# Rotary swap transfers issued by GpSimd, and gate tiles split six and twelve around retention

## The chip, the core and the metric

The kernel runs on one core of one Trainium2 chip. The metric is the device time of one launch in microseconds. Most executions of a kernel agree within 0.3%.

## The reference, cut to what matters

Two transformer blocks in a chain on 512 tokens of width 1024, in fp32. The first (gated delta rule, dilated attention and an expert layer) is left as it is. The second has two layers, and each layer does this:

```python
for l in range(2):
    proj = rmsnorm(x) @ w_in[l]            # 1024 -> everything below
    (c_q, c_kv, k_pe, sb_q, sb_k, sb_v, r_q, r_k, r_v, r_g, gate_logits) = split(proj)
    y_a = causal softmax attention from the latents c_q, c_kv, k_pe
    y_b = stick_breaking_attention(sb_q, sb_k, sb_v)   # log_sigmoid of every score
    # rotary embedding on 8 heads of 64: the two halves of a head change places
    rope(x) = concat([x1 * cos - x2 * sin, x2 * cos + x1 * sin])
    y_c = retention(rope(r_q), rope(r_k), r_v)
    y_c = silu(r_g) * head_group_norm(y_c)
    gates = sigmoid(gate_logits)           # 3 branches x 1024
    x = x + sum_b(gates[b] * (y_b @ w_branch[l, b])) @ w_out[l]
    x = x + square(relu(rmsnorm(x) @ w_up[l])) @ w_down[l]
```

## The kernel before

Activations lie transposed, features on 128 partitions and the 512 tokens along the row. A projection is a chain of *units*. A unit takes one 128x1024 weight tile and computes 128 output features: 24 matmuls of 128x512, since every fp32 product is made of three (high by high, high by low, low by high part). The tile comes in by a DMA on SP's queue into `raw`; ScalarE rounds it to its high part (`whl<-raw` on ACT), VectorE subtracts to get the low part (`whl<-raw,whl` on DVE). The units take turns in two PSUM banks, and the epilogue that reads a unit's bank is issued in the middle of the next unit, so unit n+2 can't start before the epilogue of unit n. `tm_unit` is the token-major form for v: groups of 24 matmuls with 256 columns.

Beside this main stream run *side tasks*, written as generators: the pieces of the attentions, the rotary embeddings, retention. While the program is built, a planner (`tick`, `count`, `need`, with estimated clocks of PE, ACT and DVE) lets them issue a piece between the matmuls of the units. The order of each engine's instructions is then fixed, and each engine works through its own list in order: a DMA that an engine issues stands in that list too.

The order of the main stream in a layer of block 2 is the tuple `ORDER`: the latents ("c"), some gate tiles, the up-projections ("u"), stick-breaking ("sb"), more gate tiles, retention ("r"), and the rest of the gate tiles. A number is a count of gate units out of 24; each sends its result to DRAM (`gate`), from which it is read again when the branches are merged. "sb" ends by starting the task `sticks`, which takes a softplus of every score: Exp and Ln on ACT, in bursts. "r" (`retain`) projects q and k (four units each), then v (two `tm_unit`), then adds the tasks t1 = `rope_large(q)` and t2 = `rope_large(k)`, projects the four g tiles, and adds the task `retention`, which waits for t1, t2 and the softmax attention (job "a"). It first applies Silu to g, then works through four pairs of heads. Each pair ends in a chain: a mean by a matmul, subtract, square, a matmul, Ln, Exp, two multiplies.

When the gate units are done, the kernel waits for the jobs a, b and c, splits the twelve tiles of y into high and low parts, and starts the branch units (`w_b`). These can start only when the last chain of retention is through.

`rope_large` handles two tiles at a time. For each it copies the four groups of 32 partitions to a second tile with neighbours swapped, by four DMAs of 32x512 (64 KB each), then does three VectorE operations. That is 8 tiles and 32 DMAs in a layer, 64 in all. In the before kernel ScalarE issues them.

Of the kernel before, what the change touches and what calls it, by code (L numbers as in the profile page):

```python
# [74 lines left out]
AFTER = "a"  # L75
BRANCHES = ((0, 0), (0, 2), (0, 4), (1, 0), (1, 2), (1, 4), (0, 6), (1, 6))
ORDER1 = ("da0", "k", "q", "da1", "da2", "v", "z", 16)
ORDER = ("c", 6, "u", "sb", 8, "r", 10)
CONST_GROUPS = {"base": ("ident", "ones", "freq"), "dn": ("le", "ge", "nle", "nge"), "peer": ("iota",),
                "b2": ("lt", "nlt", "nge", "b64"), "b2r": ("ntri", "nones"), "rot": ("rotm",)}  # L80

# [66 lines left out]
def layouts(x, norm_mix, w_in, dn_conv, dn_a_log, dn_dt_bias, dn_out_norm, rel_bias, w_branch_dn,  # L148
# [45 lines left out]
    for l in range(2):  # L194
# [7 lines left out]
        n = o[10]  # L202
        for i, p in enumerate(ORDER):
            if isinstance(p, int):
# [52 lines left out]
def _pick(g, a, n):  # L257

    if g == 0:
# [6 lines left out]
        + ["w_br", "w_out1", "w_route", "u", "v"]  # L266
        + [n + l for l in "01" for n in [f"w_g{i}_" if isinstance(p, int) else "w_" + p for i, p in enumerate(ORDER)]
           + ["w_b", "w_o", "w_mlp"]])
# [42 lines left out]
class Prog:  # L311
# [1691 lines left out]
    def rope_large(self, lst, deps):  # L2003

        yield from self.until(*deps)
        yield from self.need(slots=7)
        cos, sin = self.rope_tabs(1)
        for i in range(0, len(lst), 2):
            yield from self.need(slots=5)
            bs = []  # L2010
            for x in lst[i:i + 2]:
                b = self.slot()
                for j in range(4):
                    k = j ^ 1
                    self.dma(b[32 * j:32 * j + 32], x[32 * k:32 * k + 32], self.nc.scalar)
                bs.append(b)
            yield 2
            for j, b in enumerate(bs):
                x, a = lst[i + j], self.slot()
                self.tt(b, b, sin, OP.mult)  # L2020
                self.tt(a, x, cos, OP.mult)
                self.tt(a, a, b, OP.add)
                self.put(b, x)
                lst[i + j] = a
            yield
        self.put(cos, sin)

    def layer(self, l, res):
# [127 lines left out]
        n = 0  # L2156
        for p in ORDER:
            if isinstance(p, int):
# [444 lines left out]
```

## Time and profile before

| | us |
|---|---|
| median of three runs | 3950.87 (3944.65 to 3953.07) |
| profiled execution, its own time | 3947.66 |
| its span in the trace | 3945.9 |
| PE busy | 3781.2 (96%) |
| DVE busy | 2543.5 (64%) |
| ACT busy | 1537.9 (39%) |
| POOL busy | 421.8 (11%), none of it in block 2 after its start |

Block 2 takes the second half of the span, its two layers being alike. Retention's stretch in the first layer is about 2310 to 2500 us, in the second about 3270 to 3470 us. In the timeline views a row gives the start, the time that a run of like instructions took, the engine, the line (L307 is a recording helper that issues nearly everything, L582 the DMA helper), and in brackets how long the engine stood idle before it and what released it. "ACTq" rows are DMAs that ScalarE issued.

### The profile page before, as it was taken

How to read it: one execution, taken by the hardware profiler on the slowest of the kernel's cores; microseconds unless marked ns; L12 is line 12 of the kernel's file. 1: busy time of each engine (PE TensorE's matmuls, PEld its weight loads, DVE VectorE, ACT ScalarE, POOL GpSimd, SP SyncE). 2: the span in 40 equal slices, each digit the busy share in tenths (PEclk: the TensorE clock that was granted, in tenths of full speed). 3: DMA queues.
4: the chain of work that ended last, by engine and by line, in shares of the span. 5: the costliest groups of instructions: out<-in, count | busy, mean ns of one | idle time of the engine just before them, and what ended most of it. 6: DMA issues, size and time to landing. Idle time of an engine off the chain costs nothing.

```text
span 3945.9 us, 56144 instructions
## 1 busy us (share of the span) xinstructions
PE 3781.2 (96%) x21866; PEld 3228.5 (82%) x21866; DVE 2543.5 (64%) x4608; ACT 1537.9 (39%) x2392; POOL 421.8 (11%) x460
## 2 busy tenths in 40 slices
PE   9999899999999979999999998999999997999998
PEld 6777777899889979999977776688888876678886
DVE  4565755699989878888766555653345564564334
ACT  3532334244545433333343443442233353243222
POOL 1010201020333532222100000000000000000000
PEclk9999999999999999999999999999999999999999
DMA  4232524376888979999832223432233222343222
GB/s 150 80 114 87 169 94 159 126 246 198 317 317 301 380 265 348 349 347 349 292 119 94 86 84 103 152 115 97 96 115 124 72 86 86 107 155 107 96 96 80
DMA packets 260139, 666.68 MB, mean 169 GB/s; under 512 B 27316, under 2 KB 105428, under 8 KB 256800
## 3 DMA queue, kind: packets, MB, share of 16 engines
q1 hardware_dynamic: 202752, 457.19, 34.1%
q0 software_dynamic: 53328, 200.61, 13.9%
q10 hardware_dynamic: 3792, 5.28, 0.5%
q8 instruction: 172, 2.82, 0.3%
q14 instruction: 95, 0.78, 0.1%
HBM read 576.16 MB, written 81.57 MB: 167 GB/s over the span
## 4 chain that ended last, share of the span: by engine, by line
PE 55%; DVE 3%; ACT 2%; DMA 1%; issue 1%; ACTq 1%; DVEq 0%
PE bank L307 55%; DVE s L307 1%; ACT s L307 1%; DVE big L307 1%; DVE whl L307 1%; ACTq L582 1%; ACT whl L307 1%; ACT big L307 0%; DMA s<-s 0%; DVE dbl L307 0%; DMA dbl<-big 0%; DMA big<-big 0%; DMA big<-decay 0%; DMA gate<-s 0%; DVE mla_m L307 0%
## 5 line engine op out<-in xcount | busy, mean ns | idle before, releaser
L307 PE MATMUL bank<-s,whl 128*128 128x512 f32 (+1 forms) x15156 | 3276.1, 374 | 116.5 <-DVE s L307 42.9
L307 PEld LDWEIGHTS bank<-s,whl 128*128 128x128 f32 x15156 | 2759.2, 190 | 530.6 <-issue 58.9
L307 DVE TENSOR_TENSOR whl<-raw,whl 128x1024 fp32r<-128x1024 f32 x651 | 795.1, 1222 | 516.5 <-ACT whl L307 511.2
L307 ACT ACTIVATE whl<-raw 128x1024 fp32r<-128x1024 f32 x651 | 682.9, 1055 | 696.7 <-PE bank L307 358.4
L307 DVE TENSOR_TENSOR big<-bank,big 128x512 f32<-128x512 f32 (+4 forms) x264 | 174.6, 665 | 288.1 <-PE bank L307 285.4
L307 DVE TENSOR_TENSOR s<-s,s 128x1024 f16<-128x1024 f16 (+9 forms) x498 | 296.4, 616 | 32.1 <-ACT s L307 20.5
L307 ACT ACTIVATE big<-big 128x512 f32<-128x512 f32 (+2 forms) x247 | 148.3, 612 | 364.5 <-DVE big L307 309.5
L307 ACT ACTIVATE big<-bank 128x512 f32<-128x512 f32 (+3 forms) x250 | 165.0, 707 | 287.8 <-PE bank L307 179.0
L307 ACT ACTIVATE s<-bank 128x384 f32<-128x384 f32 (+5 forms) x253 | 116.8, 487 | 368.4 <-PE bank L307 357.4
L307 PE MATMUL bank<-s,s 128*128 128x128 f16 (+12 forms) x2120 | 218.9, 266 | 6.7 <-DVE s L307 6.6
L307 ACT ACTIVATE s<-s 128x384 fp32r<-128x384 f32 (+7 forms) x303 | 155.1, 526 | 175.9 <-DVE s L307 162.3
L1701 POOL DMA_INDIRECT dbl<-rows_u,s x128 | 169.3, 1322 | 325.7 <-DVE dbl L307 139.3
L307 DVE SCALAR_TENSOR_TENSOR dbl<-dbl,dbl 128x1024 f32<-128x1024 f32 x128 | 154.5, 1217 | 10.6 <-DMA dbl<-rows_u,s 8.8
L307 DVE TENSOR_TENSOR s<-s,big 128x384 f32<-128x384 f32 (+5 forms) x265 | 127.6, 485 | 33.9 <-DMA big<-wd 18.5
L307 PEld LDWEIGHTS bank<-s,s 128*128 128x128 f32 (+4 forms) x1352 | 106.5, 147 | 42.9 <-issue 27.0
L307 ACT ACTIVATE s<-big 128x512 fp32r<-128x512 f32 (+3 forms) x144 | 94.5, 668 | 109.0 <-DVE big L307 107.0
L1701 POOL DMA_INDIRECT dbl<-rows_v,s x94 | 102.0, 1085 | 259.4 <-DVE dbl L307 252.4
L307 DVE TENSOR_TENSOR s<-bank,big 128x512 f32<-128x512 f32 (+4 forms) x151 | 90.5, 609 | 52.6 <-PE bank L307 50.1
L307 PE MATMUL bank<-whl,s 128*128 128x256 f32 (+1 forms) x816 | 112.6, 298 | 12.2 <-DVE s L307 12.2
L307 PEld LDWEIGHTS bank<-whl,s 128*128 128x128 f32 x816 | 106.3, 197 | 15.7 <-DVE s L307 13.1
L307 DVE SCALAR_TENSOR_TENSOR dbl<-dbl,s,dbl 128x1024 f32<-128x1024 f32 x93 | 118.8, 1278 | 0.0
L307 DVE SCALAR_TENSOR_TENSOR big<-bank,big 128x512 f32<-128x512 f32 x68 | 46.9, 690 | 103.0 <-PE bank L307 98.9
(259 smaller groups left out, 2034.3 us busy)
## 6 DMA issues: line engine op xcount, KB each, us to landing
raw<-u SPq DMA_DIRECT2D x128, 512.0 KB
raw<-v SPq DMA_DIRECT2D x128, 512.0 KB
raw<-w_mlp SPq DMA_DIRECT2D x128, 512.0 KB
wd<-big POOLq DMA_DIRECT2D x24, 1024.0 KB
big<-wd SPq DMA_DIRECT2D x48, 512.0 KB
raw<-w_g SPq DMA_DIRECT2D x48, 512.0 KB
s<-ga SPq DMA_DIRECT2D x112, 192.0 KB
raw<-w_da SPq DMA_DIRECT2D x36, 512.0 KB
```

Of the source, the lines that this page charges most:

```text
L307: return getattr(self.eng, f)(*a, **k)
L582: (eng or self.queue).dma_start(out, in_)
L1701: self.nc.gpsimd.indirect_dma_start(buf, None, self.I[table], bass.IndirectOffsetOnAxis(ap=idx, axis=0))
```

## The change

Two lines. In `ORDER`, the gate tiles between stick-breaking and retention go from 8 to 6, and those behind retention from 10 to 12. In `rope_large`, the swap DMAs are issued by GpSimd instead of ScalarE.

```diff
-ORDER = ("c", 6, "u", "sb", 8, "r", 10)
+ORDER = ("c", 6, "u", "sb", 6, "r", 12)
@@ rope_large
                 for j in range(4):
                     k = j ^ 1
-                    self.dma(b[32 * j:32 * j + 32], x[32 * k:32 * k + 32], self.nc.scalar)
+                    self.dma(b[32 * j:32 * j + 32], x[32 * k:32 * k + 32], self.nc.gpsimd)
```

No instruction is added or dropped. The planner interleaves the side tasks anew, from the gate units ahead of retention on.

The first place is ScalarE's list in layer 0, from the swaps of q's first two tiles on, before the change. The `s`, `big` and `dbl` names are tiles of the side tasks; `big<-bank` of 384 columns is the start of a softplus.

```order
L582 DMA dbl_21144<-s_20429 32x512 x4
L582 DMA dbl_21150<-big_74 32x512 x4
L307 ACTIVATE whl<-raw 128x1024
L307 ACTIVATE big_74<-bank_80 128x512
L582 DMA big_74<-big_74 32x512 x4
L582 DMA big_75<-big_75 32x512 x4
L307 ACTIVATE big_74<-bank_82 128x384
L307 ACTIVATE big_75<-bank_81 128x384
L307 ACTIVATE s_21235<-bank_79 128x384
L307 ACTIVATE s_21236<-bank_83 128x384
```

In the change, the same engine at the same place of layer 0, around the weight splits of the second and third gate tile behind "r":

```order
L307 ACTIVATE s_20808<-s_20808 128x512
L307 ACTIVATE s_20809<-s_20809 128x512
L307 ACTIVATE whl<-raw 128x1024
L307 ACTIVATE s_21207<-bank_83 128x512
L307 ACTIVATE big_74<-bank_81 128x384
L307 ACTIVATE s_21250<-bank_79 128x384
L307 ACTIVATE s_21257<-bank_82 128x384
L307 ACTIVATE s_21258<-bank_78 128x384
L307 ACTIVATE s_21281<-bank_80 128x512
L307 ACTIVATE s_21282<-bank_83 128x512
L307 ACTIVATE whl<-raw 128x1024
```

The DMA rows are gone from it, and a weight split stands ahead of the softplus bursts where the swaps stood.

The second place is GpSimd's list in layer 0 of the change. Before, its list ends with the first row here, a reload of the residual at the start of block 2, and two rows of program end.

```order
L582 DMA s_17818<-hres 128x512
L582 DMA s_21048<-dbl_20261 32x512 x4
L582 DMA dbl_21053<-s_20331 32x512 x4
L582 DMA dbl_20261<-s_20415 32x512 x4
L582 DMA s_21154<-s_20497 32x512 x4
L582 DMA s_21211<-dbl_20261 32x512 x4
L582 DMA s_21216<-big_74 32x512 x4
L582 DMA s_21271<-big_74 32x512 x4
L582 DMA s_21276<-big_75 32x512 x4
```

All 32 swaps of the layer stand in one queue with nothing between them.

The third place is TensorE's list at the end of layer 0's retention. `bank_76<-s,whl` is the last gate unit, `bank_82<-s,whl` (in the change `bank_81<-s,whl`) the first branch unit; the others are matmuls of the side tasks. Before:

```order
L307 MATMUL bank_83<-s_21939,big_74 128x512
L307 MATMUL bank_79<-s_21907,s_20868 64x512
L307 MATMUL bank_79<-s_21909,s_20868 64x512
L307 MATMUL bank_79<-big_75,s_20926 64x384 x2
L307 MATMUL bank_78<-big_74 128x512
L307 MATMUL bank_79<-dbl_21150,s_20958 64x256
L307 MATMUL bank_79<-dbl_21360,s_20958 64x256
L307 MATMUL bank_79<-s_21941,s_20996 64x128
L307 MATMUL bank_79<-s_21943,s_20996 64x128
L307 MATMUL bank_79<-big_75,big_74 128x512
L307 MATMUL bank_81<-big_75,big_74 128x512
L307 MATMUL bank_82<-s_21970,whl 128x512
```

And in the change:

```order
L307 MATMUL bank_80<-big_75,big_74 128x512
L307 MATMUL bank_83<-big_74 128x512
L307 MATMUL bank_76<-s_18248,whl 128x512
L307 MATMUL bank_76<-s_18249,whl 128x512
L307 MATMUL bank_76<-s_18248,whl 128x512
```

```order
L307 MATMUL bank_76<-s_18284,whl 128x512
L307 MATMUL bank_76<-s_18285,whl 128x512
L307 MATMUL bank_76<-s_18284,whl 128x512
L307 MATMUL bank_79<-big_74 128x512
L307 MATMUL bank_81<-s_21968,whl 128x512
```

Before, 35 matmuls of the side tasks stand between the last gate unit and the first branch unit; in the change one does, and the others lie among the matmuls of the gate units. Retention's heads begin in the sixth of twelve gate tiles behind "r" instead of the seventh of ten. Layer 1 has the same pattern.

## Rows read from the trace of the kernel before

**Rows 1.** The page: busy time by engine; the chain that ended last.

```profile
PE 3781.2 (96%) x21866; PEld 3228.5 (82%) x21866; DVE 2543.5 (64%) x4608; ACT 1537.9 (39%) x2392; POOL 421.8 (11%) x460
PE 55%; DVE 3%; ACT 2%; DMA 1%; issue 1%; ACTq 1%; DVEq 0%
```

**Rows 2.** Timeline of PE, layer 0: start us, us, instructions, idle before them.

```profile
2325.15 4.59 PE L307 MATMUL bank<-whl,s 128*128 128x256 f32 x24 [4.48 <-DVE s L307]
...
2386.16 6.11 PE L307 MATMUL bank<-s,whl 128*128 128x512 f32 x18 [11.72 <-DVE s L307]
...
2407.96 16.85 PE L307 MATMUL bank<-s,whl 128*128 128x512 f32 x72 [0.44 <-DVE dbl L307]
...
2478.53 0.95 PE L307 MATMUL bank<-s,s 64*128 64x128 f32 x4 [1.28 <-DVE s L307]
...
2490.80 1.13 PE L307 MATMUL bank<-big,big 128*128 128x512 f32 x2 [1.12 <-ACT big L307]
2493.36 1.12 PE L307 MATMUL bank<-big,big 128*128 128x512 f32 x2 [1.44 <-ACT big L307]
2496.45 0.79 PE L307 MATMUL bank<-s,whl 128*128 128x512 f32 x1 [1.96 <-ACT s L307]
2498.04 12.15 PE L307 MATMUL bank<-s,whl 128*128 128x512 f32 x43 [0.81 <-DVE s L307]
```

**Rows 3.** Timeline of PE, layer 1, the two longest waits.

```profile
3286.44 5.14 PE L307 MATMUL bank<-whl,s 128*128 128x256 f32 x24 [4.48 <-DVE s L307]
...
3352.98 5.73 PE L307 MATMUL bank<-s,whl 128*128 128x512 f32 x18 [15.48 <-DVE s L307]
```

**Rows 4.** Chain of waits, 2370 to 2400 us: start us, us, what.

```profile
2377.59 1.94 DMA s<-s
...
2383.30 0.96 ACT whl L307
2384.28 1.23 DVE whl L307
2385.51 0.60 DVE s L307
```

**Rows 5.** Timeline of ACT, layer 0: softplus burst, swaps, table load.

```profile
2314.31 0.52 ACT L307 ACTIVATE big<-big 128x384 f32<-128x384 f32 x1
...
2320.88 1.99 ACT L307 ACTIVATE whl<-raw 128x1024 fp32r<-128x1024 f32 x2
...
2362.64 5.01 ACTq L582 DMA_DIRECT2D big<-big  x8
2371.78 0.96 ACT L307 ACTIVATE big<-bank 128x384 f32<-128x384 f32 x2 [8.57 <-DVE big L307]
...
2374.37 5.10 ACTq L582 DMA_DIRECT2D s<-s  x8
...
2428.64 1.28 ACT L555 ACT_TABLE_LOAD   x1
```

**Rows 6.** Timeline of DVE: waits for transfers, block 2 and block 1.

```profile
2358.62 0.69 DVE L307 TENSOR_TENSOR dbl<-dbl 128x512 f32<-128x512 f32 x1 [4.04 <-DMA dbl<-s]
...
3322.37 0.69 DVE L307 TENSOR_TENSOR dbl<-dbl 128x512 f32<-128x512 f32 x1 [5.95 <-DMA dbl<-s]
...
481.39 0.69 DVE L307 TENSOR_TENSOR s<-s,s 128x512 f32<-128x512 f32 x1 [3.24 <-DMA s<-og]
```

**Rows 7.** Windows, layer 0: busy PE, PEld, DVE, ACT, POOL; PEclk; DMA share; GB/s.

```profile
2386.00:2390.00 4.00, 3.84 (x9) 3.07 (x10) 3.26 (x8) 2.43 (x4) 0.00 (x0) 0.51 0.00 0
2498.00:2502.00 4.00, 3.96 (x9) 3.14 (x10) 4.00 (x7) 4.00 (x8) 0.00 (x0) 0.50 0.77 226
```

**Rows 8.** Timeline of POOL, block 1: DMAs that GpSimd issues.

```profile
478.44 0.54 POOL L582 DMA_DIRECT2D s<-og  x1 [0.55 <-DVE dbl L307]
...
598.78 3.19 POOL L582 DMA_DIRECT2D big<-gd  x6
...
1460.97 0.56 POOL L582 DMA_DIRECT2D rope<-s  x1 [6.24 <-ACT s L307]
```

## The prediction, made before the changed kernel ran

> **What bounds the kernel now.** I read the page first. TensorE is busy 96% of the span and is the largest piece of the chain that ended last; no other engine has over 64% [rows 1]. The change adds no work to TensorE and takes none away, so it can only move TensorE's idle time and its clock. That idle time is the next thing to look for, in the timeline of PE through retention's stretch in both layers. In layer 0 it is in four places. One wait of 4.48 us stands in v's projection. One of 11.72 us stands ahead of a unit behind retention's projections. Two waits of about 0.5 us follow, of which one is shown. And the end of retention has five waits of 1.28, 1.12, 1.44, 1.96 and 0.81 us, 6.6 in sum; two more there, under 0.3 us each, are left aside [rows 2]. Layer 1 repeats the pattern row by row, but its long wait is 15.48 us [rows 3]. Together that is 23.7 and 27.5 us, 51.2 in all.
>
> What ends the long wait is read from the chain of waits and the timeline of ACT. The transfer of a swap arrives, ScalarE then works through a softplus burst, reaches the high part of the next weight tile at 2383.30, VectorE makes the low part at 2384.28 and the epilogue at 2385.51, and only that frees the bank that TensorE wants [rows 4]. Just ahead ScalarE issued eight swap DMAs in 5.01 us, waited 8.57 us until it could read the scores of the burst, and issued eight more in 5.10 us [rows 5]. Ten microseconds of an in-order engine went into issuing, with the weight split queued behind.
>
> The long waits also cost clock. Behind the one of layer 0, and at the start of the branch units, the granted clock is 0.51 and 0.50, the lower of the two levels (1.2 and 2.4 GHz) [rows 7]. Its price comes from the rows. Seventy-two matmuls take 16.85 us at the full clock, 0.234 each. So 18 should take 4.2 and took 6.11 in layer 0 and 5.73 in layer 1, and 43 should take 10.1 and took 12.15 [rows 2, 3]. That is 1.9, 1.5 and 2.1 us.
>
> **Part 1, the swaps leave ScalarE.** Per layer, 32 DMAs at 0.63 us (5.01 over eight) are 20 us of ScalarE's list [rows 5]. Most of that lies beside TensorE's work and costs nothing; the part that ends late is the long wait. With the DMA rows gone, the weight split stands ahead of the bursts and waits for nothing but its own tile and ScalarE's turn. I take the 11.72 and the 15.48 as gone: −27.2 us.
>
> GpSimd does nothing in block 2, so its issues cost no work of its own. Its price for an issue is 0.54 us, and six in a row took 3.19 [rows 8]: the 32 of a layer take 17 us. A transfer that it issues at 478.44 is used at 481.39, 2.95 us later [rows 6, 8]. So a pair of tiles needs 8 × 0.54 + 3 = 7.3 us, a little more than one unit (24 × 0.234 = 5.6 us). The rows before show two waits of VectorE for swaps, 4.04 and 5.95 us [rows 6], with no idle row of TensorE at either. So a swap that is late by a few microseconds has cover.
>
> The Trainium skill, "SBUF — State Buffer", section "SBUF: two separate sides", speaks against this part: GpSimd writes the descriptors of its DMAs itself, and can't while VectorE runs an operation in a mode with two ports. The Trainium skill, "SBUF — State Buffer", section "Who interferes with whom", says that TENSOR_TENSOR has no such mode. The row that bears on it is an issue of 0.56 us in a stretch where VectorE runs TENSOR_TENSOR [rows 8], so the trace agrees with the second sentence and no row of it shows the first.
>
> **Part 2, the gate split.** The two gate units taken from ahead of "r" move everything of retention 11 us earlier against the softplus bursts. So the wait in v's projection meets a later unit of that projection, but the same queue: a burst of softplus from 2314.31 on, then two weight splits until 2322.87 [rows 5]. I keep it, at 4.0 for 4.48: −0.5 a layer.
>
> At the end two more gate units lie beside the last heads of retention. In the order of the change one matmul of the side tasks stands between the last gate unit and the first branch unit, instead of 35. The waits of 1.28, 1.12 and 1.44 us are then inside the units and covered; what can't be covered is the last chain itself (Ln, Exp, then the high and low parts of y), 1.96 + 0.81 = 2.8 us [rows 2]. That is −3.8 a layer, −7.7 in all.
>
> Two places may get worse. First, the cosine and sine tables of k are fetched again on SP's queue while VectorE waits for them, and behind the six operations of that pair stands an epilogue of a gate unit. The bounds are 0 (as at the two covered waits) and 5.95 us, the longest wait of VectorE for such a transfer [rows 6]. Second, the Silu of the g tiles needs a table load of 1.28 us [rows 5], and another back to Exp and Ln, now nearer to a weight split. Its bounds are 0 and 4.48 us, what the burst in v's projection costs [rows 2]. I take 2.0 for each, nearer to zero because TensorE ran through both waits of VectorE before: +4.0 a layer, with the two small waits of 0.5 us gone in return, so +3.0.
>
> **Sum.** Idle: −27.2 − 1.0 − 7.7 + 6.0 = −29.9; with the small waits left aside, about −31. Clock: −1.9 − 1.5 at the long waits; at the branch units I expect most of 2.1 back in layer 0, and more than that in layer 1 where it also falls in the chain, together about −5. That is −8. In all −39 us. Against the profiled execution of 3947.66 us this gives 3909; it lies 3.2 us under the median of 3950.87, within the spread of the runs, and the median less 39 is 3911.9, of which I keep 3911.
>
> **The rivals.**
>
> *The issuer doesn't matter.* The wait could be the softplus bursts' own: the split that ends it comes behind eight activations as well as behind the DMAs [rows 4, 5]. Then the long waits stay, by another releaser, and only the tail improves: 7.7 us of idle time, 8.6 with the small waits left aside, and the 5 of clock at the branch units, 13.6 in all: 3937. For it: the wait of 4.48 us has a burst and no DMA in it. Against it: ten microseconds of issuing between 2362 and 2380. The Trainium skill, "DMA: Bandwidth & Descriptors", section "Issuing engines are not separate DMA queues", is on this rival's side: starting transfers on several engines saves only the sequencer's time to issue, usually small against the transfer. Here eight issues hold ScalarE for 5.01 us [rows 5] and the wait for the data behind them is 1.94 us [rows 4], so by the trace the issue is the larger part.
>
> *A new wait takes the old one's place.* The two new places cost near their upper bounds, 5 to 6 us each, not 2. Then +15 of idle time against my sum and the clock of two more waits, 4: 3911.9 + 19, about 3931.
>
> *Better.* If the softplus burst in v's projection is covered too and the new waits don't come, only 2.8 a layer stays of the 51.2: 46 us of idle time (47 with the small ones) and 12 of clock, 3892.
>
> *Slower: GpSimd's issues stretch.* This kernel would do so if an issue waits for the VectorE operations beside it. The place is the last pairs of k: between the ninth issue and the use of the last pair lie about five units, 28.5 us with the side work, in which 23 issues of p us and a landing of 4.5 (between 2.95 and 5.95 [rows 6]) must fit. The pair is late by 23p + 4.5 − 28.5, nothing at 0.54. About 2 us of lateness are covered, and part 1 and 2 gain 20 a layer, so the sign turns where 23p = 46, at p = 2.0. If each issue waited for two operations like a weight's low part (1.23 [rows 4]), p would be 3.0, the pair 45 us late, and each layer would lose 22.5: 3996. The Trainium skill, "SBUF — State Buffer", section "A bandwidth-pool intuition that's wrong (but worth ruling out)", gives about 3,100 ns for such a DMA beside a locking operation of VectorE, against 620 ns alone; taken for p, that would be 48 us late and about 4002. Against it: the issue row of 0.56 us, and that the rows of VectorE in this stretch are TENSOR_TENSOR [rows 4, 6, 8].
>
> **How the numbers follow.** The forecast has 62%. The issuer that doesn't matter has 10%, the new waits 10%, the better case 4%, the slower one 8%. A last 6% is for the slower mechanism at its point of balance, around p = 2, with a time within 0.2% of before. About 0.2%, 8 us, is what a measurement of this kernel can tell from no change. So faster has 0.62 + 0.10 + 0.10 + 0.04 = 0.86, same 0.06, slower 0.08. The range goes from 3896, where both new waits are zero and a little of the burst is covered too, to 3937, the first rival: the better, the same and the slower cases are left out, 18%.
>
> **What would show it.** After the change no wait of TensorE over 6 us in retention's stretch; the 4.48 still there at the end of a softplus burst; one wait of about 2 + 0.8 us before the branch units, without a clock of 0.5 behind the places where the long waits were; POOL rows of 32x512 swaps at 0.5 to 0.6 us each, VectorE waiting for them no longer than 6 us. The rival of the issuer is right if a wait over 8 us stands before the same units with ACT's burst as what holds the split. The prediction is wrong in its main term if POOL's issues take over 1.1 us each, or if the epilogue behind k's tables holds TensorE longer than the 5.95 us taken as its bound.

## The result, and the profile after

The changed kernel takes 3899.6 us (median of four, 3895.3 to 3900.8), against 3947.8 for the kernel before, run beside it. The ratio is 0.9882 with a 95% interval of 0.9869 to 0.9894: 1.2% faster, by 48 us. The forecast was 3911, in a range of 3896 to 3937.

Two lines of the page after answer to [rows 1]: TensorE has the same 21866 instructions, is busy 8.8 us less, and its share of the chain that ended last is 58% instead of 55%.

```profile
PE 3772.4 (97%) x21866; PEld 3221.4 (83%) x21866; DVE 2541.1 (65%) x4608; ACT 1536.9 (39%) x2392; POOL 457.6 (12%) x524
PE 58%; DVE 2%; ACT 2%; issue 1%; DMA 0%; DVEq 0%; ACTq 0%
```

In the timeline of PE after, these are all the waits of layer 0 in the stretch that [rows 2] shows of before, and the two longest ahead of the branch units of layer 1. Columns as in [rows 2].

```profile
2319.91 10.40 PE L307 MATMUL bank<-whl,s 128*128 128x256 f32 x72 [3.00 <-ACT s L307]
...
2375.05 4.33 PE L307 MATMUL bank<-s,whl 128*128 128x512 f32 x18 [0.95 <-DVE big L307]
...
2388.11 1.61 PE L307 MATMUL bank<-s,whl 128*128 128x512 f32 x6 [0.53 <-ACT s L307]
...
2395.65 0.49 PE L307 MATMUL bank<-dbl,s 128*128 128x512 f32 x1 [0.21 <-ACT dbl L307]
...
2396.38 1.08 PE L307 MATMUL bank<-s,s 128*128 128x512 f32 x5 [0.23 <-DVE s L307]
...
2473.86 0.50 PE L307 MATMUL bank<-s,whl 128*128 128x512 f32 x1 [1.96 <-ACT s L307]
2475.46 24.76 PE L307 MATMUL bank<-s,whl 128*128 128x512 f32 x96 [1.09 <-DVE s L307]
...
3263.18 10.25 PE L307 MATMUL bank<-whl,s 128*128 128x256 f32 x72 [3.00 <-ACT s L307]
...
3319.05 4.36 PE L307 MATMUL bank<-s,whl 128*128 128x512 f32 x18 [1.83 <-DVE big L307]
```

The waits of 11.72 and 15.48 us [rows 2, 3] have become 0.95 and 1.83. The wait in v's projection is 3.00 instead of 4.48. Of the five at the end of retention the last two are left, 1.96 and 1.09.

The time is accounted for best from where block 2 starts on, since the first block is the same code in both kernels. Its first long run of matmuls starts 3.8 us earlier in the profiled execution of after than in that of before:

```profile
1995.51 17.26 PE L307 MATMUL bank<-s,whl 128*128 128x512 f32 x64 [9.78 <-DVE whl L307]
```

(before), and

```profile
1991.75 17.00 PE L307 MATMUL bank<-s,whl 128*128 128x512 f32 x64 [9.78 <-DVE whl L307]
```

(after). In the fourteen traces of this study that start lies anywhere between 1985.8 and 1997.7, so 3.8 us is scatter. From it to the end of the span block 2 takes 1950.4 us before and 1906.2 after, 44.2 less. The idle time of TensorE in it, added up from all rows of its timeline, falls from 58.6 to 22.5: 36.1. Nearly all of the rest, 8.1, is clock: PE's busy time times (1 − PEclk), added over windows of 4 us through retention's stretch in both layers (2270 to 2530 and 3230 to 3502 us), falls from 14.8 to 7.0, by 7.8. The table has the same sums for the experiments, each ratio against the kernel before, run beside it; the last three columns are from one trace each.

| kernel | time, us (median) | ratio to before | block 2 | PE idle in it | lost to clock |
|---|---|---|---|---|---|
| before | 3947.8 | | 1950.4 | 58.6 | 14.8 |
| changed | 3899.6 | 0.9882 [0.9869, 0.9894] | 1906.2 | 22.5 | 7.0 |
| changed, once more | 3897.8 | 0.9881 [0.9865, 0.9896] | 1906.1 | 22.2 | 7.3 |
| GpSimd issues, split 8/10 | 3922.3 | 0.9941 [0.9923, 0.9959] | 1933.0 | 39.0 | 19.8 |
| ScalarE issues, split 6/12 | 3920.0 | 0.9930 [0.9911, 0.9949] | 1926.9 | 36.1 | 12.3 |
| SP issues, split 6/12 | 3899.6 | 0.9878 [0.9855, 0.9900] | 1905.0 | 23.1 | 6.3 |
| two DMAs for each swap | 3898.8 | 0.9881 [0.9865, 0.9898] | 1906.9 | 23.8 | 6.3 |
| four DMAs for each swap | 3955.9 | 1.0027 [1.0017, 1.0037] | 1965.9 | 63.7 | 24.2 |
| split 7/11 | 3908.7 | 0.9907 [0.9891, 0.9924] | 1917.6 | 33.0 | 11.3 |
| split 5/13 | 3893.2 | 0.9865 [0.9848, 0.9881] | 1902.3 | 25.0 | 5.0 |
| split 5/13, once more | 3895.7 | 0.9870 [0.9855, 0.9885] | 1902.5 | 25.1 | 5.2 |
| split 4/14 | 3905.6 | 0.9894 [0.9879, 0.9909] | 1910.3 | 29.2 | 4.9 |
| split 6/12, branch units of two attentions first | 3899.0 | 0.9879 [0.9863, 0.9896] | 1904.8 | 22.1 | 5.7 |
| split 5/13, branch units of two attentions first | 3914.0 | 0.9914 [0.9901, 0.9928] | 1918.5 | 32.2 | 9.5 |

### The profile page after: what moved, and what is told of

The parts are those of the page before. It is cut to its first block, busy times and chain, and to the rows that moved or that the text cites. A ratio compares the mean times of both kernels' runs of the same rounds, so it can differ in the third digit from the quotient of the medians.

```text
span 3898.0 us, 56154 instructions
## 1 busy us (share of the span) xinstructions
PE 3772.4 (97%) x21866; PEld 3221.4 (83%) x21866; DVE 2541.1 (65%) x4608; ACT 1536.9 (39%) x2392; POOL 457.6 (12%) x524
## 4 chain that ended last, share of the span: by engine, by line
PE 58%; DVE 2%; ACT 2%; issue 1%; DMA 0%; DVEq 0%; ACTq 0%
PE bank L307 58%; DVE s L307 1%; ACT s L307 1%; DVE big L307 1%; ACT whl L307 0%; DMA big<-rope 0%; DVE whl L307 0%; ACT L555 0%; ACT big L307 0%; DVE mla_m L307 0%; DVE dbl L307 0%; ACT dbl L307 0%; DVE bank L307 0%; DVEq L2598 0%; DVEq L307 0%
## 5 line engine op out<-in xcount | busy, mean ns | idle before, releaser
L307 ACT ACTIVATE s<-bank 128x384 f32<-128x384 f32 (+6 forms) x263 | 122.0, 489 | 414.1 <-PE bank L307 406.6
L307 PE MATMUL bank<-s,s 128*128 128x128 f16 (+10 forms) x2102 | 209.2, 260 | 4.6 <-DVE s L307 4.6
L582 POOL DMA_DIRECT2D s<-dbl x16 | 7.9, 500 | 1319.6 <-PE bank L307 1319.6
L307 PEld LDWEIGHTS bank<-s,s 32*32 32x32 f32 (+5 forms) x1334 | 104.4, 146 | 37.0 <-issue 26.2
L307 ACT ACTIVATE s<-big 128x512 fp32r<-128x512 f32 (+2 forms) x136 | 90.6, 677 | 106.7 <-DVE big L307 104.7
L307 PE MATMUL bank<-s,big 32*32 32x32 f32 (+6 forms) x960 | 121.2, 283 | 1.7 <-ACT big L307 1.3
```

The source lines that it names most:

```text
L307: return getattr(self.eng, f)(*a, **k)
L582: (eng or self.queue).dma_start(out, in_)
```

## Experiments: the two parts apart

**The issuer alone.** The split stays at 8 and 10:

```diff
-ORDER = ("c", 6, "u", "sb", 6, "r", 12)
+ORDER = ("c", 6, "u", "sb", 8, "r", 10)
```

(This diff and those below are against the changed kernel.)

> Only the issuer changes (GpSimd), the gate split stays 8 and 10; every engine's list but ScalarE's and GpSimd's is that of before. Theory (ScalarE's 20 us of issuing a layer ends the long wait): the waits of 11.72 and 15.48 us shrink under 4 us each, the end of retention keeps its waits (about 7 us a layer), the time falls by 25 to 32 us, near 3920. Rival (the softplus burst alone holds the weight split): a wait of 8 us or more stays at the same unit, the time falls by under 8 us.

It took 3922.3, 24 us less than before, just short of the 25 to 32 expected. Its timeline of PE has these waits in v's projection and at the unit where the long wait was, in layer 0 and in layer 1:

```profile
2316.16 5.49 PE L307 MATMUL bank<-whl,s 128*128 128x256 f32 x24 [4.48 <-DVE s L307]
2371.16 6.96 PE L307 MATMUL bank<-s,whl 128*128 128x512 f32 x18 [4.56 <-DVE s L307]
...
3327.91 6.50 PE L307 MATMUL bank<-s,whl 128*128 128x512 f32 x18 [4.76 <-DVE s L307]
```

The long wait shrinks by 7.2 and 10.7 us, but doesn't go, and stays above the 4 us expected. The chain of waits ahead of it, in order of time (start us, us, what), tells what is left:

```profile
2354.89 3.65 DMA big<-big
...
2365.96 2.34 ACT s L307 x5
2368.30 0.96 ACT whl L307
...
2369.28 1.23 DVE whl L307
2370.51 0.61 DVE s L307
```

The last of the softplus burst's activations (five in the second row), then the weight split, its low part and the epilogue: the tail of [rows 4] without the issues ahead of it. A swap's transfer is still in the chain (first row): VectorE waits 3.08 us for it, works off the pair and then reads the scores, and ScalarE, idle for 7.82 us, begins the burst only at 2361.39. So the first rival had a part of it right: with no issue left in ScalarE's list, the burst and what the burst waits for still cost TensorE 4.6 us. And the clock did not improve: 18 matmuls behind a wait of 4.56 us take 6.96 us, no less than the 6.11 behind 11.72 [rows 2]. Over the stretch this kernel loses more to the clock than before, 19.8 for 14.8; why more was not settled.

**The split alone.**

```diff
-                    self.dma(b[32 * j:32 * j + 32], x[32 * k:32 * k + 32], self.nc.gpsimd)
+                    self.dma(b[32 * j:32 * j + 32], x[32 * k:32 * k + 32], self.nc.scalar)
```

> Only the gate split changes (6 and 12), ScalarE issues the swaps. Theory (the two parts are separate): waits of about 8 to 16 us a layer stay between v's projection and retention's heads, the end of retention keeps only about 3 us, the time falls by 12 to 18 us, near 3934. Rival (two units more of distance are enough by themselves): no wait over 5 us, the time within 8 us of the changed kernel's 3900.

It took 3920.0, 27 us less than before, more than the 12 to 18 expected. The wait in v's projection is 3.00 in each layer, as in the changed kernel; with the issuer alone it stayed at 4.48. The end of retention has 3.0 us left in each layer, as expected. Between v's projection and the heads the waits are 7.1 us in layer 0 (a little under the 8 to 16 expected) and 10.2 in layer 1 in sum, of which these are the ones of layer 0 above 1 us:

```profile
2371.82 7.33 PE L307 MATMUL bank<-s,whl 128*128 128x512 f32 x24 [1.77 <-DVE s L307]
2384.16 6.93 PE L307 MATMUL bank<-s,whl 128*128 128x512 f32 x18 [5.01 <-DVE big L307]
```

In its chain of waits ScalarE's issuing is a piece of its own: eight DMAs between two parts of one burst, with the weight split behind the second.

```profile
2369.11 1.39 ACT s L307 x3
...
2370.57 0.60 ACTq L582
2371.20 0.61 ACTq L582
...
2375.13 1.09 ACT s L307 x2
2376.22 0.96 ACT whl L307
```

So both causes are real, and either part alone leaves the other's wait. In block 2 the issuer alone gives 17.4 us, the split alone 23.5, both 44.2: nearly the sum (40.9). In idle time the two overlap (19.6 and 22.5 against 36.1), and in clock it is the other way: the issuer alone loses 5.0 more than before, the split alone 2.5 less, both 7.8 less.

## Experiments: the queue that issues

**SP in GpSimd's place.**

```diff
-                    self.dma(b[32 * j:32 * j + 32], x[32 * k:32 * k + 32], self.nc.gpsimd)
+                    self.dma(b[32 * j:32 * j + 32], x[32 * k:32 * k + 32], self.nc.sync)
```

> The changed kernel with the swaps on SP's queue instead of GpSimd's, where weight tiles, gate results and the cosine and sine tables are queued too. Theory (any engine that isn't ScalarE does, since weight tiles are fetched several units ahead): within 6 us of the changed kernel. Rival (SP's in-order list stands still while a swap waits for its tile, and the weight loads behind it come late): TensorE waits for raw tiles or their high parts, 5 to 15 us a layer, 10 to 30 us slower than the changed kernel.

3899.6, the changed kernel's time; block 2 at 1905.0. So nothing of the gain hangs on GpSimd; what counts here is that the issuer isn't ScalarE. SP needs 0.59 us for one, GpSimd 0.50 and ScalarE 0.60 (median by line, DMAs of 32x512 from one SBUF tile to another).

**The fourth rival's price.** Each swap in pieces of 8 rows, four times the issues for the same bytes (and in the second kernel of 16 rows, twice):

```diff
-                    self.dma(b[32 * j:32 * j + 32], x[32 * k:32 * k + 32], self.nc.gpsimd)
+                    for p in range(0, 32, 8):
+                        self.dma(b[32 * j + p:32 * j + p + 8], x[32 * k + p:32 * k + p + 8], self.nc.gpsimd)
```

> The changed kernel with each swap cut in four DMAs of 8x512 on GpSimd: 128 issues a layer instead of 32, the same bytes. At 0.5 us each the formula of the prediction has p at 2.0 per swap: the last pair 22 us late (23 x 2.0 + 4.5 - 28.5), some 20 us of wait a layer, about 40 to 50 us slower than the changed kernel, near 3945. Rival (an issue costs by its rows, so that a quarter of a swap costs a quarter of 0.5 us, or the pairs have more cover than five units): within 6 us of the changed kernel.

> The changed kernel with each swap cut in two DMAs of 16x512 on GpSimd: 64 issues a layer, p = 1.0 us per swap. By the formula of the prediction the last pair is in time (23 x 1.0 + 4.5 - 28.5 = -1): within 6 us of the changed kernel. Rival (every 0.5 us more per swap costs in proportion, as from 32 to 128 issues, where it cost 56 us): 15 to 20 us slower, near 3918.

Four pieces took 3955.9: slower than before the change. An issue costs nearly the same whatever its rows (0.508 us with 8, 0.484 with 16, 0.496 with 32), so p is 4 × 0.508 = 2.0. By line, the swaps of both layers, the two largest of four groups, min/median/max ns:

```profile
L582 POOL DMA_DIRECT2D s<-big x96: 502/508/511, 2376.6 to 3372.8; - x96
L582 POOL DMA_DIRECT2D s<-dbl x64: 502/508/536, 2331.4 to 3348.3; - x64
```

Its chain of waits in the stretch is GpSimd's issuing, and TensorE waits for the pairs one after the other:

```profile
2369.67 6.13 POOL s L582 x13
...
2382.10 4.05 DMA s<-big
...
2386.43 5.25 POOL s L582 x11
```

```profile
2373.85 8.56 PE L307 MATMUL bank<-s,whl 128*128 128x512 f32 x24 [3.62 <-DVE s L307]
2392.84 7.68 PE L307 MATMUL bank<-s,whl 128*128 128x512 f32 x24 [10.43 <-DVE s L307]
2406.17 6.45 PE L307 MATMUL bank<-s,whl 128*128 128x512 f32 x18 [5.66 <-DVE big L307]
```

The prediction's formula gives 22 us of lateness at p = 2.0 and, less 2 of cover, 20 of wait a layer; the idle time of block 2 is 41.2 above the changed kernel's, 20.6 a layer. What it left out is the clock, 17.2 us more (24.2 against 7.0), so the sign turns somewhat below p = 2. Two pieces (p = 1.0) took 3898.8, as the formula says: the cover of five units is used up only beyond that.

## Experiments: how far the gates should move

Two more splits, then a third:

```diff
-ORDER = ("c", 6, "u", "sb", 6, "r", 12)
+ORDER = ("c", 6, "u", "sb", 7, "r", 11)
```

> The changed kernel with seven and eleven gate units. In its order 24 matmuls of the side tasks stand between the last gate unit and the first branch unit. Theory: it lies between the two splits; the end of retention waits about 5 us a layer, v's projection and the unit behind it keep the 4.5 us waits of the kernel with only the issuer changed, which has the same distance but one unit; 8 to 18 us slower than the changed kernel, 3908 to 3918. Rival (the wait behind v's projection hangs on the burst's place by one unit): it goes as in the changed kernel, and only 3 to 5 us are lost.

3908.7, at the near end of the expectation. The end of retention waits 5.9 us in layer 0, and the wait where the long one was is back at 4.08 and 5.41: it hangs on the burst's place by one unit. The wait in v's projection was expected at 4.5 and is 2.21.

> The changed kernel with five gate units ahead of retention and thirteen behind it. In its order 80 matmuls of the side tasks stand between the last gate unit and the first branch unit, where the changed kernel has one: retention's heads begin later although it has more units behind it. Theory (what counts is how many of retention's matmuls lie among gate units): waits of about 8 to 14 us a layer at the end of retention instead of 3, lower clock behind them, 15 to 30 us slower than the changed kernel, 3915 to 3930. Rival (each unit behind retention covers more of it): 3900 or less.

3893.2 where 3915 to 3930 was expected: a miss. The order of the matmuls had been read as if those that no gate unit surrounds were lost time. They take as long as anywhere; what costs is the chain of ACT and DVE between them. That the pairs of heads run side by side here and cover one another's chains is the likely reason, and was not tested. In its timeline of PE the end of layer 0's retention has eight waits, 7.45 us in sum, of which the last three are

```profile
2470.32 1.13 PE L307 MATMUL bank<-big 128*128 128x512 f32 x2 [1.44 <-ACT big L307]
2473.41 0.79 PE L307 MATMUL bank<-s,whl 128*128 128x512 f32 x1 [1.96 <-ACT s L307]
2475.01 45.29 PE L307 MATMUL bank<-s,whl 128*128 128x512 f32 x191 [0.80 <-DVE s L307]
```

Against that the waits behind v's projection are gone, the one in it is 1.63, and the clock is lost for less time. These don't add up to a lead: over block 2 the idle time is 2.5 us more than in the changed kernel and the clock's loss 2.0 less, while block 2 is 3.9 shorter. With the same 8978 matmuls TensorE is busy there for 1864.5 us instead of 1870.7; the clock explains 2.0 of that, and what shortens the rest was not settled.

> The changed kernel once more, beside the next three on one chip: 3896 to 3903, its ratio to the kernel before 0.987 to 0.990.

> Five and thirteen gate units once more. If its lead over the changed kernel (6 us, of which 4 lie in block 2) is real: 3 to 8 us under the changed kernel in the same call. If it was the scatter of the first block: within 2 us.

> The changed kernel with four and fourteen gate units. In its order 74 matmuls of the side tasks stand in one piece late in retention, much as with five and thirteen. If distance from the softplus bursts goes on paying: 3893 or less. If it is used up, since the waits that are left belong to the end of retention (about 7.5 us a layer with five and thirteen): 3892 to 3898.

On one chip the changed kernel took 3897.8 (0.9881, 0.9865 to 0.9896), five and thirteen 3895.7 (0.9870, 0.9855 to 0.9885): the intervals overlap. In block 2 the lead is the same in both pairs of traces, 1906.2 and 1906.1 against 1902.3 and 1902.5, so some 4 us of 3900 are probably real, and too little for these runs to show. Four and fourteen takes 3905.6, outside both expectations (3893 or less, 3892 to 3898): the waits at the end of retention stay and smaller ones come in the middle of it.

**The last chain covered.** What is left at the end with six and twelve is the last chain, 1.96 + 1.09 us a layer. The branch units of the other two attentions don't need it:

```diff
-        self.wait(*(job[x] for x in "abc"))
-        ys = [[self.hilo(t) for t in y] for y in (ya, yb, yc)]
+        self.wait(*(job[x] for x in "ab"))
+        ys = [[self.hilo(t) for t in y] for y in (ya, yb)]
...
             for b in range(3):
+                if b == len(ys):
+                    self.wait(job["c"])
+                    ys.append([self.hilo(t) for t in yc])
                 w = self.get()
```

> The changed kernel, but the branch units of the softmax and the stick-breaking attention start without waiting for retention; only the first branch unit that reads retention's result waits for it and splits its tiles. Theory (what is left at the end is retention's last chain, 1.96 + 1.09 us a layer): that wait shrinks to about 1 us, the high and low part of the first tile, and the clock behind it stays up in layer 0; 4 to 8 us faster than the changed kernel, near 3894. Rival (the wait moves to the third branch unit, or the splits of eight tiles ahead of it take its place): within 3 us of the changed kernel.

3899.0, no gain. In its timeline of PE the wait has moved:

```profile
2472.75 10.96 PE L307 MATMUL bank<-s,whl 128*128 128x512 f32 x47 [0.29 <-DVE s L307]
2484.76 0.50 PE L307 MATMUL bank<-s,whl 128*128 128x512 f32 x1 [1.05 <-ACT s L307]
2486.95 23.22 PE L307 MATMUL bank<-s,whl 128*128 128x512 f32 x94 [1.69 <-DVE s L307]
```

0.29 + 1.05 + 1.69 is 3.03, the same sum, 48 matmuls later. The 11 us of branch work are filled on ScalarE by eight splits of y that now stand ahead of the chain and by three loads of its tables, since Sigmoid comes between the chain's Ln and Exp and what went before:

```profile
2469.90 2.18 ACT L307 ACTIVATE s<-big 128x512 fp32r<-128x512 f32 x4
2471.98 2.19 ACT L307 ACTIVATE s<-s 128x512 fp32r<-128x512 f32 x4
...
2478.13 1.28 ACT L555 ACT_TABLE_LOAD   x1
2479.42 0.69 ACT L307 ACTIVATE big<-bank,eps 128x512 f32<-128x512 f32 x1
...
2481.74 1.28 ACT L555 ACT_TABLE_LOAD   x1
```

> Five and thirteen gate units, and the branch units of the other two attentions not waiting for retention. Its order lets 44 matmuls of the side tasks in one piece ahead of the last branch units. If retention's last chains are what is left (7.5 us a layer) and 22 us of branch work can cover half: 6 to 10 us under five and thirteen alone, near 3885. If the wait only moves to the first branch unit that reads retention's result, as with six and twelve: within 3 us of five and thirteen alone.

With five and thirteen the same edit took 3914.0 (0.9914, 0.9901 to 0.9928), 18 us more than without it, a miss of both expectations. In block 2 the idle time is 7.1 us more than without it and the clock's loss 4.3 more, of 16.0; the end of layer 0's retention waits 11 us in sum instead of 7.45. Why the edit lengthens these waits was not settled. No version tried beats the changed kernel by more than the runs can tell.

## Why the prediction came out right, step by step

The time, the sign and the range held, and the mechanism was the one forecast. The sizes of its terms were less good than their sum.

- **The long waits, −27.2 expected.** They are gone; the 0.95 and 1.83 us that stand at that place now hang on k's tables and are counted below. But the prediction gave all of it to part 1, the issuer. The issuer alone takes 17.9 of it (11.72 to 4.56, 15.48 to 4.76), and the rest goes only when part 2 moves the burst by two units as well. The shares depend on the order: of all waits between v's projection and the heads (29.2 in both layers) the issuer alone takes 19.9, the split alone 11.8, both 24.6. The step that failed is "With the DMA rows gone, the weight split stands ahead of the bursts": the kernel with only part 1 has the burst ahead of the split. The forecast for both parts held because both were made.
- **The wait in v's projection, −1.0 expected.** It went from 4.48 to 3.00 in each layer, −3.0; the split alone gives the same 3.00.
- **The end of retention, −7.7 expected.** From 7.1 a layer, with the two small waits that the prediction left aside, to 3.05: −8.1. What stays is Ln, Exp and the split of y, as named, at 3.05 for 2.8.
- **The two new waits, +8.0 expected, less the small ones.** They came where they were looked for, at 0.95 and 1.83 for the tables of k, and 1.0 and 0.9 around the Silu: 4.6 in sum. Of these last, 0.4 in each layer stand behind the Silu's table loads; 0.5 in each come just ahead of them (at 2388.11, the first load at 2389.34), and what they wait for was not settled. The chain of waits of after shows the first:

```profile
2355.02 4.32 DMA big<-rope
...
2363.33 3.15 DVE s L307 x6
2366.50 0.60 ACT s L307
2367.09 0.96 ACT whl L307
...
2374.30 0.60 DVE big L307
```

 The transfer of the tables takes 4.32 us of the chain, VectorE stands idle for 4.57 us (5.46 in layer 1), and TensorE pays 0.95 (1.83) when the epilogue in the last row comes late. The second rival, with 5 to 6 us at each place, is out.
- **Clock, −8 expected.** 7.8 measured, most of it where it was forecast. By place, the sum of the table falls from 3.3 to 0 behind the long waits (−3.4 expected; 18 matmuls now take 4.33 and 4.36), from 7.8 to 4.3 at the end of retention and the branch units (−5 expected), and from 3.6 to 2.7 in v's projection (nothing expected). At the branch units of layer 0 none came back: the first row here, of after with the columns of [rows 7], has 0.55 where before had 0.50. In layer 1 it did in part (second row). The changed kernel's second trace has it the other way round, with 1.2 lost there in layer 0 instead of 2.9, and 2.9 in layer 1 instead of 1.4. So which layer gets its clock back differs between two executions of one kernel, and only the sum (7.0 and 7.3) can be compared.

```profile
2474.00:2478.00 4.00, 2.91 (x7) 2.11 (x8) 3.96 (x8) 4.00 (x9) 0.00 (x0) 0.55 1.01 345
...
3418.00:3422.00 4.00, 2.91 (x8) 2.07 (x9) 3.97 (x8) 4.00 (x9) 0.00 (x0) 0.73 0.94 322
```

- **GpSimd's issues.** 0.50 us each, where the row before had 0.54. Of the 64, 57 stand beside a TENSOR_TENSOR of VectorE and take 0.498 at most; the other seven have no VectorE operation beside them and take 0.535 at most. VectorE never waits over 1 us for a swap. In the timeline of POOL after, layer 0:

```profile
2330.46 2.01 POOL L582 DMA_DIRECT2D s<-dbl  x4 [400.24 <-PE bank L307]
...
2341.78 1.96 POOL L582 DMA_DIRECT2D dbl<-s  x4 [7.36 <-DVE dbl L307]
```

 The slower rival had its threshold about right, and its condition does not occur here. The rule of the Trainium skill, "SBUF — State Buffer", section "SBUF: two separate sides", is neither shown nor refuted: the only operations beside these issues are TENSOR_TENSOR. The Trainium skill, "DMA: Bandwidth & Descriptors", section "Issuing engines are not separate DMA queues", says that the sequencer's time is all that another issuer saves, and that it is "usually small relative to the DMA itself". For a single DMA the trace does not speak against it: one issue on ScalarE takes 0.60 us, and the wait for a transfer behind it 1.94 [rows 4]. But eight in a row held ScalarE for 5.01 us [rows 5] with a weight split behind them, and moving the issues was worth 17.4 us by itself.

With the small waits of before gone too (2.0 in both layers), the idle terms come to −27.2 − 3.0 − 8.1 + 4.6 − 2.0 = −35.7, of the 36.1 measured, where −31 was forecast: the wait in v's projection gave 2 us more than taken, and the new waits cost 3.4 less. The clock was −8 and measured −7.8. So block 2 gained 44.2 where 39 was forecast. The medians differ by 48; the further 4 us lie outside block 2 in the one pair of profiles, in code that is the same in both kernels, and there is no second trace of before to tell whether the medians hold the same scatter.

Two slips in the prediction's slower rival change nothing: at p = 3.1 its formula gives 47.3 us of lateness, not 48, and at p = 3.0 a loss of 45 − 2 − 20 = 23 a layer, not 22.5.

## What to carry to other kernels

A DMA issue is an instruction of the engine that issues it, and on an engine that also computes in order it delays everything behind it; move it to one whose list nobody waits for, and check that the list there can issue all of it within the cover. A wait often has two causes queued in one engine: taking away one shortens it, and only the edits tried apart and together show what each does alone and how much of it they share. Matmuls between main units are not lost time; count the chains of the other engines between them that nothing runs beside.

## What was not expected of the hardware

- Among the waits that cost clock, a longer one does not cost more. Behind a wait of 4.56 us 18 matmuls took 6.96 us, behind 11.72 us 6.11 and behind 15.48 us 5.73; behind 0.95 us they took 4.33, close to the 4.2 of the full clock.
- A DMA that GpSimd issues costs it 0.508 us with 8 rows of 512, 0.484 with 16 and 0.496 with 32: the issue, not the bytes, is paid.
- The first block, the same code in all fourteen traces, ends at times that lie 12 us apart (1985.8 to 1997.7), a quarter of what the change gains.
